# Gate products of a recurrent block: three reduced-precision products of split operands in place of full-precision matmuls, on a two-block model with attention, recurrence, long convolution and experts

## The chip, the cores and the metric

One core of a Trainium2 chip runs the whole forward pass of two model blocks for one sequence of 256 tokens (width 1024). Its engines work side by side, each on its own queue: TensorE (PE; its weight loads are listed as PEld), VectorE (DVE), ScalarE (ACT), GpSimd (POOL) and SyncE (SP, which issues most transfers). The metric is the device time of one execution in microseconds; lower is better.

## The reference, cut to what matters

The first block has two layers (windowed attention with an MLP, then a gated recurrence with an MLP), the second a mix of three token mixers and an expert layer. The change is in the gates of the recurrence. `x` there is 256 x 1536, cut into 16 blocks of 96 channels, and each block has a 96 x 96 matrix for each of two gates and two directions:

```python
def rg_lru(x, w_a, b_a, w_x, b_x, lam, reverse):
    xb = x.reshape(B, S, N_RNN_BLOCKS, RNN_BLOCK_W)
    r = sigmoid(einsum("bsni,nij->bsnj", xb, w_a).reshape(B, S, D_RNN) + b_a)
    i = sigmoid(einsum("bsni,nij->bsnj", xb, w_x).reshape(B, S, D_RNN) + b_x)
    log_a = -LRU_C * r * softplus(-lam)
    a = exp(log_a)
    u = sqrt(-expm1(2.0 * log_a)) * (i * x)
    ...                       # linear scan over time of (a, u)

def recurrent_block(h, w_in, conv_w, conv_b, ..., w_out):
    xr, gate = split(h @ w_in, 2)
    xr = centred_depthwise_conv(xr, conv_w, conv_b)
    y = rg_lru(xr, forward) + rg_lru(xr, reverse)
    return (y * gelu(gate)) @ w_out
```

The second thing the change touches is the spectra of the long-convolution filters of the second block (`Kre`, `Krz`, `Kim`), which depend on weights alone and are computed early.

## The kernel before

Large products are made of three fp32r matmuls each: both operands are split into a high part, rounded by a copy to fp32r on ScalarE, and a low part, the difference, made on VectorE; `mm3` (L388) adds high x high, high x low and low x high. Weights come through one stream `W` (class `Stream`): SyncE loads items of 1 MB into five staging buffers, `split_to` (L219 ScalarE, L224 VectorE) splits them in halves of 1024 columns into four pairs of buffers, `next` hands them out in a fixed order. A scheduler orders each engine's instructions by program order and readiness, except in attention, where TensorE's order is as written. GpSimd issues the small loads (`GP.dma_start`) and does few operations.

The recurrent block (`recurrent`, from L1452) works on four groups of 384 channels, in three tiles of 128 channels by 256 tokens. For each group:

- `gin(g)`: for each tile, 48 matmuls 128x256 of split input and weights give x and the gate branch in one PSUM bank; ScalarE copies them out (L1476, L1477, L1484, L1485), VectorE does the convolution taps (L1479) and the gelu (L1486, L1488). `xr[g]` holds the three x tiles.
- `gates(g)`: 96-channel blocks do not line up with 128-channel tiles, so an output tile `mt` needs the x tiles in `PAIRS[mt]`: the first needs x tiles 0 and 1, the middle one all three, the last 1 and 2. For each direction, output tile and gate, L1503 issues a full-precision (f32) matmul per pair, of the loaded blocks `BD[g % 2]` with zeros around them: 28 in a group, each of which the trace lists as two instructions. Then ScalarE takes two biased tanh, an exp and a tanh for each tile and direction (L1506 to L1509) and a square (L1512); VectorE multiplies (L1513, L1514). After all of them come square roots (L1523), scans over time (L1529, L1531) and the product with the gelu, split into `yH` and `yL` (L1536, L1537).
- `gout(g - 1)`: 36 products 128x512 of the previous group's `yH`, `yL` with output weights, into four accumulator banks. The last group's follow at the end.

The general banks (`gen`) are three in rotation, so a gate product can start only when the bank three before it has been read. For the last group, gates and what follows run tile by tile (`pieces`).

`load_bd(g)` loads a group's gate blocks by 20 small DMAs on GpSimd's queue (L1430) into one of two buffers `BD[0]`, `BD[1]`; groups 0 and 1 are loaded ahead of the first MLP, 2 and 3 after `gates(0)` and `gates(1)`. `run_late(ins)` runs four operations of 128x1024 on the residual (`affine`, L905 and L908), in group 1; they read the tiles `lng`, `lnb`. The filter spectra stay in `Kre`, `Krz`, `Kim` from the end of attention until the second block's convolution. `channel_terms` runs in the middle of the first MLP.

## Time and profile before

| | |
|---|---|
| Time of three runs | 1211.99, 1214.86 (median), 1220.63 us |
| Profiled execution | 1219.98 us, of which the span from first to last instruction is 1218.2 us |
| TensorE busy | 1128.1 us, 93% of the span |
| VectorE busy | 771.6 us, 63% |
| ScalarE busy | 552.4 us, 45% |
| GpSimd busy | 104.2 us, 9% |
| HBM traffic | 315.27 MB read, 1.09 MB written, 260 GB/s over the span |
| Mean granted clock of TensorE | 0.974 |

Busy time is an average over stages: TensorE at 93% does not say which engine ends each stage. So the rows below are cut by stage. The recurrent block runs from about 350 to 528 us of the span, the first MLP from about 153 to 339, the second from about 541. A matmul's duration overlaps that of the next; what it costs is the distance between two starts.

### The profile page before, as it was taken

To read this page: it belongs to the slowest core of one execution; us is meant where nothing else is said; L and a number is where in the kernel's file an instruction comes from. 1 tells how busy PE (TensorE), PEld (TensorE's weight loads), DVE (VectorE), ACT (ScalarE), POOL (GpSimd) and SP (SyncE) were. 2 spreads that over 40 slices of the span, in tenths; PEclk is the share of its full clock that TensorE was granted. 3 is DMA by queue.
4 is the path that set the end of the run, shared out by engine and by line. 5 is a ranking of instruction groups with operands and counts; after the bars stand their busy time and mean duration, and the time that the engine had idled before them with its cause. 6 is when DMAs were issued, how large, how long until landed. Compare 5 with 4: busy or idle time off the path is not lost. (4 is left out here: it accounts for less than half of the span.)

```text
span 1218.2 us, 17320 instructions
## 1 busy us (share of the span) xinstructions
PE 1128.1 (93%) x6610; PEld 822.0 (67%) x6610; DVE 771.6 (63%) x1448; ACT 552.4 (45%) x935; POOL 104.2 (9%) x177
## 2 busy tenths in 40 slices
PE   5999699999989999979999999899999997989884
PEld 3657598988866577558889989899987543334321
DVE  4588688878575786588778879878798511101003
ACT  2456344454467777745345547644656211011101
POOL 6000170000013210010000000100000000000000
PEclk9999889999999999989999999999999899999998
DMA  9988498988694572478779766653346769999993
GB/s 285 327 320 302 175 311 295 337 293 306 205 277 125 168 198 69 143 279 323 261 267 321 270 211 208 209 174 129 100 143 239 284 249 419 417 413 419 420 411 124
DMA packets 147075, 317.58 MB, mean 261 GB/s; under 512 B 8402, under 2 KB 97730, under 8 KB 133672
## 3 DMA queue, kind: packets, MB, share of 16 engines
q1 hardware_dynamic: 139768, 304.17, 69.9%
q0 software_dynamic: 7216, 12.22, 3.2%
q8 instruction: 54, 0.88, 0.3%
q14 instruction: 37, 0.30, 0.1%
HBM read 315.27 MB, written 1.09 MB: 260 GB/s over the span
## 5 line engine op out<-in xcount | busy, mean ns | idle before, releaser
L219 ACT ACTIVATE wh<-stg 128x1024 fp32r<-128x1024 f32 x236 | 241.2, 1042 | 190.2 <-issue 71.9
L224 DVE TENSOR_TENSOR wl<-stg,wh 128x1024 fp32r<-128x1024 f32 x233 | 277.0, 1207 | 75.8 <-ACT wh L219 73.0
L391 PE MATMUL gen<-hH,wh 128*128 128x256 f32 x704 | 198.5, 282 | 4.3 <-ACT hH L851 3.0
L393 PE MATMUL gen<-hH,wl 128*128 128x256 f32 x704 | 197.2, 281 | 5.0 <-DVE wl L224 5.0
L392 PE MATMUL gen<-hL,wh 128*128 128x256 f32 x704 | 196.3, 279 | 1.3 <-DVE hL L855 1.3
L391 PEld LDWEIGHTS gen<-hH,wh 128*128 128x128 f32 x704 | 133.7, 190 | 12.1 <-ACT hH L851 5.7
L393 PEld LDWEIGHTS gen<-hH,wl 128*128 128x128 f32 x704 | 133.8, 190 | 7.9 <-DVE wl L224 7.8
L392 PEld LDWEIGHTS gen<-hL,wh 128*128 128x128 f32 x704 | 133.5, 190 | 3.2 <-POOL zp L1458 1.1
L391 PE MATMUL acc<-wh,mH 128*128 128x512 f32 x256 | 101.3, 396 | 0.0
L393 PE MATMUL acc<-wh,mL 128*128 128x512 f32 x256 | 100.7, 393 | 0.0
L392 PE MATMUL acc<-wl,mH 128*128 128x512 f32 x256 | 100.5, 392 | 0.0
L468 DVE SCALAR_TENSOR_TENSOR adav<-stg,csil,adav 128x1024 f32<-128x1024 f32 (+2 forms) x56 | 79.3, 1415 | 10.2 <-DMA stg<-in_ada_w_dram 9.4
L2423 PE MATMUL mmi<-stg,mhT 128*32 128x512 f32 (+2 forms) x256 | 69.6, 599 | 7.7 <-SPq L2486 3.9
L2395 PE MATMUL mgu<-stg,wh 128*32 128x512 f32 (+2 forms) x256 | 66.6, 648 | 5.9 <-DMA stg<-in_moe_w_up_dram 5.9
L2395 PE MATMUL mgu<-stg,wl 128*32 128x512 f32 (+2 forms) x256 | 65.1, 595 | 7.2 <-DMA stg<-in_moe_w_up_dram 7.2
L2400 DVE SCALAR_TENSOR_TENSOR mhid<-mgu,mws,mhid 128x512 f32<-128x512 f32 x7 | 5.3, 750 | 93.8 <-PE mgu L2395 93.8
L1503 PE MATMUL gen<-xr,bd 128*128 128x256 f32 (+1 forms) x224 | 60.3, 410 | 1.4 <-DVE xr L1479 1.4
L2428 ACT ACTIVATE wh<-mmi 128x512 fp32r<-128x512 f32 x14 | 8.4, 598 | 111.7 <-PE mmi L2423 111.7
L2423 PEld LDWEIGHTS mmi<-stg,mhT 128*32 128x32 f32 (+2 forms) x256 | 20.2, 129 | 54.5 <-issue 36.2
L2429 DVE TENSOR_TENSOR wl<-mmi,wh 128x512 fp32r<-128x512 f32 x14 | 9.7, 692 | 74.0 <-ACT wh L2428 74.0
L391 PEld LDWEIGHTS acc<-wh,mH 128*128 128x128 f32 x256 | 48.1, 188 | 11.7 <-ACT mH L1310 0.8
L393 PEld LDWEIGHTS acc<-wh,mL 128*128 128x128 f32 x256 | 48.1, 188 | 11.0 <-issue 0.8
(597 smaller groups left out, 2160.0 us busy)
## 6 DMA issues: line engine op xcount, KB each, us to landing
stg<-in_ada_w_dram SPq DMA_DIRECT2D x72, 1024.0 KB, 6.1
stg<-in_mlp_w_dram SPq DMA_DIRECT2D x64, 1024.0 KB, 6.5
stg<-in_moe_w_up_dram SPq DMA_DIRECT2D x32, 1024.0 KB, 16.3
stg<-in_moe_w_gate_dram SPq DMA_DIRECT2D x32, 1024.0 KB, 15.2
stg<-in_moe_w_down_dram SPq DMA_DIRECT2D x32, 1024.0 KB, 18.8
stg<-in_w_in_dram SPq DMA_DIRECT2D x20, 1024.0 KB, 5.4
stg<-in_rnn_w_in_dram SPq DMA_DIRECT2D x12, 1024.0 KB, 6.3
stg<-in_attn_w_in_dram SPq DMA_DIRECT2D x8, 768.0 KB, 10.4
```

What stands on the lines that cost most here:

```text
L219: nc.scalar.activation(h, t[:, sl], AF.Copy)
L224: sub()
L391: PE.matmul(o, ah, bh, start=first, stop=False)
L392: PE.matmul(o, ah, bl, start=False, stop=False)
L393: return PE.matmul(o, al, bh, start=False, stop=last)
L468: V.scalar_tensor_tensor(acc, tv[:, j, :], col[:, k:k + 1], acc, op0=OP.mult, op1=OP.add)
L1503: PE.matmul(pv[c0:c1, q, :], BD[g % 2][:, q, d, o:o + c1 - c0], xr[g][:, kt, :], start=(i == 0), stop=True, skip_group_check=True)
L2395: PE.matmul(ps[sl], gx[c][:, k, o + sl.start:o + sl.stop], t[:, 512 * k:512 * k + 512], start=first, stop=last)
L2400: V.scalar_tensor_tensor(hid, got[1], WS[w], hid, op0=OP.mult, op1=OP.mult)
L2423: PE.matmul(ps[h][sl], hT[:, 2 * c + k, sl], t[:, 1024 * k + 512 * h:1024 * k + 512 * h + 512], start=c == 0 and k == 0, stop=c == 1 and k ...
L2428: SC.activation(yH[:, h, :], ps[h], AF.Copy)
L2429: V.tensor_sub(yL[:, h, :], ps[h], yH[:, h, :].bitcast(F32))
```

## The change

The gate matrices and the x tiles are split like the other operands, and the gate products become three fp32r products each.

- `split_bd(g)`: ScalarE copies the loaded blocks (two halves of 1280 columns) to `BDH`, GpSimd subtracts to get `BDL`, then the next group's load is issued. `BD`, `BDH`, `BDL` exist once each. Group 0's split stands at the end of `channel_terms`, the others' after the second tile of `gin(g)`.
- x is split after each tile of `gin`: copies on ScalarE, the low part on GpSimd for the first two tiles and on VectorE for the third. A fourth, mixed tile holds channels 32 to 127 of x tile 0 and 0 to 31 of x tile 2, so that the middle output tile needs two contractions and not three. The split tiles live in the buffers `lng` and `lnb`; `run_late` therefore moves to the first tile of group 0.
- The layout `SLOT` gives every piece the full 128 output columns (640 columns in all), and an output tile takes two pieces (`MINE`): one over 128 rows and, for the first and last tile, one over 64 rows, in different halves of the array; six pieces a group. The products of output tiles 0 and 2 alternate, then tile 1 follows.
- `gout(g - 1)` becomes a generator: its first 6 of 12 steps are placed after direction 0 of `gates(g)`, the rest after direction 1.
- The spectra lie in one tile `KK`, which is written to DRAM (`parked`) when they are complete and read back after the recurrent block; its 10 KB a partition are free in between.

The diff without the unchanged and the purely renamed parts:

```diff
@@ -947,9 +947,18 @@
     sks = ExitStack()
     sxp = ctx.enter_context(tc.tile_pool(name="sx", bufs=1, side="right", reuse_waits="tile"))
     skp = sks.enter_context(tc.tile_pool(name="sk", bufs=1, side="right", reuse_waits="tile"))
-    Kre = skp.tile([128, 2, 2, 256], F32, name="Kre")
-    Krz = skp.tile([128, 2, 256], F32, name="Krz")
-    Kim = skp.tile([128, 2, 2, 256], F32, name="Kim")
+
+    def filters(pool):
+
+
+        KK = pool.tile([128, 2560], F32, name="KK")
+        return (KK, KK[:, 0:1024].rearrange("p (k o c) -> p k o c", k=2, o=2),
+                KK[:, 1024:1536].rearrange("p (o c) -> p o c", o=2),
+                KK[:, 1536:2560].rearrange("p (k o c) -> p k o c", k=2, o=2))
+
+    KK, Kre, Krz, Kim = filters(skp)
+    parked = ctx.enter_context(tc.tile_pool(name="park", bufs=1, space=bass.MemoryType.DRAM)).tile(
+        [128, 2560], F32, name="parked")
...
         hps.close()
+        GP.dma_start(parked, KK)
+        sks.close()
...
@@ -1405,29 +1416,33 @@
         V.tensor_scalar(hb[:, 0], CV("b_a"), 0.5, None, op0=OP.mult)
         V.tensor_scalar(hb[:, 1], CV("b_x"), 0.5, None, op0=OP.mult)
         yield
-
-
-    SLOT, o = {}, 0
-    for key, c0, c1 in (((0, 0), 0, 128), ((1, 0), 96, 128), ((1, 1), 0, 128), ((0, 1), 0, 64), ((2, 1), 64, 128),
-                        ((2, 2), 0, 128), ((1, 2), 0, 32)):
-        SLOT[key] = (o, c0, c1)
-        o += c1 - c0
+        split_bd(0)
+        yield
+
+
+    SLOT = {(0, 0): 0, (1, 1): 128, (2, 2): 256, (1, 0): 384, (1, 2): 384, (0, 1): 512, (2, 1): 512}
     bds = ExitStack()
     bdp = bds.enter_context(tc.tile_pool(name="bd", bufs=1, reuse_waits="tile"))
-    BD = []
-    for b_ in range(2):
-        bd = bdp.tile([128, 2, 2, 576], F32, name=f"bd{b_}")
-        GP.memset(bd[:, 0], 0.0)
-        GP.memset(bd[:, 1], 0.0)
-        BD.append(bd)
+    BD = bdp.tile([128, 2, 2, 640], F32, name="bd")
+    GP.memset(BD[:, 0], 0.0)
+    GP.memset(BD[:, 1], 0.0)
+    BDH = bdp.tile([128, 2, 2, 640], F32R, name="bdH")
+    BDL = bdp.tile([128, 2, 2, 640], F32R, name="bdL")
+
+    def split_bd(g):
+        for q in range(2):
+            SC.activation(BDH[:, q], BD[:, q], AF.Copy)
+            GP.tensor_sub(BDL[:, q], BD[:, q], BDH[:, q].bitcast(F32))
+        if g < 3:
+            load_bd(g + 1)
 
     def load_bd(g):
         for q, n in enumerate(("rnn_w_a", "rnn_w_x")):
             src = A[n][0].rearrange("d n i j -> i n d j")
 
             def put(key, p0, p1, c0, c1, b, i0, j0):
...
     load_bd(0)
-    load_bd(1)
...
+                if g == 0 and j == 0:
+                    run_late(ins)
+                if j == 0:
+                    xs[g] = [lnp.tile([128, D], F32, name=n, bufs=1).bitcast(F32R).rearrange(
+                        "p (j n) -> p j n", j=4) for n in ("lng", "lnb")]
+                xH, xL = (v[:, j, :] for v in xs[g])
+                SC.activation(xH, u, AF.Copy)
+                (V if j == 2 else GP).tensor_sub(xL, u, xH.bitcast(F32))
+
+                mH, mL = (v[:, 3, :] for v in xs[g])
+                if j == 0:
+                    SC.activation(mH, u, AF.Copy)
+                    GP.tensor_sub(mL, u, mH.bitcast(F32))
+                if j == 2:
+                    SC.activation(mH[0:32], u[0:32], AF.Copy)
+                    V.tensor_sub(mL[0:32], u[0:32], mH[0:32].bitcast(F32))
+                if g and j == 1:
+                    split_bd(g)
+
+        def gates(g, between):
             pieces = [slice(0, 3)] if g < 3 else [slice(i, i + 1) for i in range(3)]
             tr, ti, aa = [[rw.tile([128, 3, 256], F32, name=n) for _ in range(2)] for n in ("tr", "ti", "aa")]
+
+            MINE = {0: ((0, 0, 128, 0), (384, 0, 64, 1)), 1: ((128, 0, 128, 1), (512, 0, 128, 3)),
+                    2: ((256, 0, 128, 2), (384, 64, 128, 1))}
+
+            def products(ps, d, mts):
+
+                for q in range(2):
+                    for part in range(2):
+                        for x, y_ in ((BDH, 0), (BDH, 1), (BDL, 0)):
+                            for mt in mts:
+                                o, p0, p1, j = MINE[mt][part]
+                                PE.matmul(ps[mt][:, 256 * q:256 * q + 256], x[p0:p1, q, d, o:o + 128], xs[g][y_][p0:p1, j, :],
+                                          start=part == 0 and x is BDH and not y_, stop=part == 1 and x is BDL)
+
             for pc in pieces:
                 for d in range(2):
-                    for mt in range(pc.start, pc.stop):
-                        ps = gen()
-                        pv = ps.rearrange("p (m n) -> p m n", m=2)
-                        c = 12 * d + 3 * g + mt
-                        for q in range(2):
-                            for i, kt in enumerate(PAIRS[mt]):
-                                o, c0, c1 = SLOT[kt, mt]
-                                PE.matmul(pv[c0:c1, q, :], BD[g % 2][:, q, d, o:o + c1 - c0], xr[g][:, kt, :],
-                                          start=(i == 0), stop=True, skip_group_check=True)
-                        r, u, e = tr[d][:, mt], ti[d][:, mt], aa[d][:, mt]
-                        SC.activation(r, pv[:, 0, :], AF.Tanh, bias=hb[:, 0, c:c + 1], scale=0.5)
-                        SC.activation(u, pv[:, 1, :], AF.Tanh, bias=hb[:, 1, c:c + 1], scale=0.5)
-                        SC.activation(e, r, AF.Exp, bias=sn4[:, c:c + 1], scale=sn4[:, c:c + 1])
-                        SC.activation(r, r, AF.Tanh, bias=sp4[:, c:c + 1], scale=sp4[:, c:c + 1])
+                    ps = {}
+                    for banks in ((0, 2), (1,)) if g < 3 else ((pc.start,),):
+                        for mt in banks:
+                            ps[mt] = gen()
+                        products(ps, d, banks)
+                        for mt in banks:
+                            c = 12 * d + 3 * g + mt
+                            pv = ps[mt].rearrange("p (m n) -> p m n", m=2)
+                            r, u, e = tr[d][:, mt], ti[d][:, mt], aa[d][:, mt]
+                            SC.activation(r, pv[:, 0, :], AF.Tanh, bias=hb[:, 0, c:c + 1], scale=0.5)
+                            SC.activation(u, pv[:, 1, :], AF.Tanh, bias=hb[:, 1, c:c + 1], scale=0.5)
+                            SC.activation(e, r, AF.Exp, bias=sn4[:, c:c + 1], scale=sn4[:, c:c + 1])
+                            SC.activation(r, r, AF.Tanh, bias=sp4[:, c:c + 1], scale=sp4[:, c:c + 1])
+                    next(between, None)
 
                     q = rw.tile([128, 3, 256], F32, name="sq", bufs=1)
                     last = SC.activation(q[:, pc], aa[d][:, pc], AF.Square)
                     V.scalar_tensor_tensor(tr[d][:, pc], q[:, pc], 1.0, tr[d][:, pc], op0=OP.add, op1=OP.mult)
                     V.scalar_tensor_tensor(ti[d][:, pc], ti[d][:, pc], 1.0, xr[g][:, pc], op0=OP.add, op1=OP.mult)
-            if g < 2:
-                load_bd(g + 2)
...
-            for m, t, h in order:
+            for n, (m, t, h) in enumerate(order):
+                if n == 6:
+                    yield
                 wh, wl = cur[m // 2](m % 2)
                 ts, hs = slice(128 * t, 128 * t + 128), slice(512 * h, 512 * h + 512)
                 mm3(y[t][h], (H[:, m - 3 * g, ts], L[:, m - 3 * g, ts]), (wh[:, hs], wl[:, hs]), m == 0, m == 11)
 
         for g in range(4):
-            ins = gin(g)
-            if g == 1:
-                run_late(ins)
-            gates(g)
-            if g:
-                gout(g - 1)
-        gout(3)
+            gin(g)
+            out = gout(g - 1) if g else iter(())
+            gates(g, out)
+            for _ in out:
+                pass
+        for _ in gout(3):
+            pass
...
+    sks = ExitStack()
+    skp = sks.enter_context(tc.tile_pool(name="sk2", bufs=1, side="right", reuse_waits="tile"))
+    KK, Kre, Krz, Kim = filters(skp)
+    GP.dma_start(KK, parked)
```

## Rows read from the trace of the kernel before

**Rows 1.** Busy time by stage: stretch, length, busy us (instructions), clock, DMA share, GB/s
```profile
350.50:527.50 177.00, 171.60 (x1006) 117.99 (x1010) 123.21 (x191) 127.39 (x234) 27.14 (x48) 1.00 0.55 169
...
368.80:384.40 15.60, 15.60 (x66) 5.56 (x64) 6.04 (x9) 11.82 (x26) 4.91 (x9) 1.00 0.64 208
...
384.40:428.10 43.70, 41.61 (x246) 29.16 (x246) 32.50 (x44) 34.02 (x61) 17.03 (x30) 1.00 0.45 128
428.10:471.50 43.40, 42.88 (x246) 29.67 (x245) 29.16 (x46) 31.42 (x56) 3.81 (x7) 1.00 0.55 162
...
471.50:490.60 19.10, 17.44 (x148) 16.71 (x146) 17.90 (x28) 13.91 (x22) 0.00 (x0) 1.00 0.33 110
250.00:335.00 85.00, 85.00 (x541) 73.22 (x540) 63.40 (x92) 38.67 (x46) 1.35 (x2) 1.00 0.78 264
```

The columns after the length are TensorE, its weight loads, VectorE, ScalarE, GpSimd.

**Rows 2.** Page, costliest groups: line, operation, shape, count, busy us, mean ns, idle before
```profile
L1503 PE MATMUL gen<-xr,bd 128*128 128x256 f32 (+1 forms) x224 | 60.3, 410 | 1.4 <-DVE xr L1479 1.4
```

**Rows 3.** Timeline of TensorE: start us, length us, line, operation, shape, count
```profile
480.00 0.29 PE L391 MATMUL gen<-hH,wh 128*128 128x256 f32 x1
...
483.87 0.28 PE L392 MATMUL gen<-hL,wh 128*128 128x256 f32 x1
...
498.50 8.21 PE L1503 MATMUL gen<-xr,bd 128*64 128x256 f32 x32
...
506.99 0.40 PE L392 MATMUL acc<-wl,yH 128*128 128x512 f32 x1
...
514.92 0.40 PE L393 MATMUL acc<-wh,yL 128*128 128x512 f32 x1
```

**Rows 4.** ScalarE: two groups by line, and its timeline in group 3's gates
```profile
L219 ACT ACTIVATE wh<-stg 128x1024 fp32r<-128x1024 f32 x36 | 37.8, 1059 | 18.8 <-PE gen L392 12.0 <-PE acc L393 4.7 <-DMA stg<-in_mlp_w_dram 2.1
...
L1476 ACT ACTIVATE zp<-gen 128x256 f32<-128x256 f32 x12 | 4.4, 370 | 0.4 <-PE gen L393 0.4
...
501.61 0.46 ACT L1507 ACTIVATE ti<-gen,hb 128x256 f32<-128x256 f32 x1
...
503.61 0.47 ACT L1507 ACTIVATE ti<-gen,hb 128x256 f32<-128x256 f32 x1
```

**Rows 5.** VectorE: two groups by line, 343 to 528 us
```profile
L224 DVE TENSOR_TENSOR wl<-stg,wh 128x1024 fp32r<-128x1024 f32 x35 | 42.3, 1218 | 8.6 <-ACT wh L219 8.2
...
L1537 DVE TENSOR_TENSOR yL<-tr,yH 128x256 fp32r<-128x256 f32 x3 | 1.3, 417 | 0.5 <-ACT yH L1536 0.5
```

**Rows 6.** Timelines of GpSimd and VectorE; line L855 on both: ns min/median/max, starts
```profile
147.45 3.69 POOL L855 TENSOR_TENSOR hL<-tv,hH 128x512 fp32r<-128x512 f32 x2 [16.26 <-ACT hH L851]
...
147.72 2.30 DVE L224 TENSOR_TENSOR wl<-stg,wh 128x1024 fp32r<-128x1024 f32 x1
...
L855 POOL TENSOR_TENSOR hL<-tv,hH x6: 1262/1267/2238, 147.5 to 539.9; 128x512 fp32r<-128x512 f32 x6
L855 DVE TENSOR_TENSOR hL<-tv,hH x6: 677/682/1183, 152.7 to 543.1; 128x512 fp32r<-128x512 f32 x6
```

**Rows 7.** Timelines of ScalarE and VectorE around the gates of group 0
```profile
371.69 1.00 DVE L1479 SCALAR_TENSOR_TENSOR xr<-zp,chv,xr 128x256 f32<-128x256 f32 x2
...
386.84 0.83 ACT L1512 ACTIVATE sq<-aa 128x768 f32<-128x768 f32 x1
```

**Rows 8.** Timeline of ScalarE in group 3's gates; in brackets the idle time before
```profile
500.44 0.47 ACT L1506 ACTIVATE tr<-gen,hb 128x256 f32<-128x256 f32 x1 [3.99 <-PE gen L1503]
```

**Rows 9.** Stretches as in rows 1, and a TensorE wait from its timeline
```profile
346.00:349.00 3.00, 0.97 (x7) 0.58 (x5) 2.44 (x7) 2.20 (x6) 0.38 (x1) 1.00 0.95 360
...
149.00:152.00 3.00, 0.18 (x2) 0.00 (x1) 2.79 (x6) 2.17 (x6) 3.00 (x2) 0.51 0.00 0
...
533.00:536.00 3.00, 2.46 (x11) 2.10 (x12) 2.65 (x9) 1.58 (x4) 0.00 (x0) 0.50 0.96 325
...
533.54 0.88 PE L842 MATMUL gen<-csm,xnat 128*128 128x128 f32 x3 [4.23 <-DVE bmv L878]
```

9 lines of the change are left out of this document (3 added, 6 removed).

## The prediction

> **What bounds the kernel now.** I read the busy time by stage first. The recurrent block, the stage that the change edits, is 177.0 us long, and TensorE is busy for 171.6 of them; ScalarE for 127.4, VectorE for 123.2, GpSimd for 27.1 [rows 1]. TensorE is the bound, at full clock, and the other two have some 50 us to spare each. Next, the group of the gate products: 112 full-precision matmuls, each listed as two instructions, keep TensorE busy for 60.3 us [rows 2]. Last, the timeline, for the pitch at which matmuls follow each other (a duration overlaps the next one's). The 128x256 products of split operands run from 480.00 to 483.87 in 34 steps: 3.87 / 34 = 0.114 us each. The gate products of the last group, 32 instructions in 8.21 us, take 0.257 us each, so 0.514 a matmul. The output products, 128x512, run from 506.99 to 514.92 in 34 steps: 0.233 us each [rows 3].
>
> **The gate products.** The new loop issues, for each of four groups and two directions, 3 column blocks x 2 gates x 2 pieces x 3 products = 36 matmuls, 288 in all. At 0.114 us they take 32.8 us in place of 60.3: TensorE is rid of 27.5 us, or 6.9 a group (15.1 to 8.2). 96 of the 288 contract over 64 rows only, a form for which before has no row. If two of them ran at once (72 can pair, in groups 0 to 2) that would save 36 x 0.114 = 4.1 us more; if each cost as much as a full-precision one, 96 x (0.514 - 0.114) = 38.4 us would be lost. I take 0.114: they move the same 256 columns in the same format.
>
> **What the split adds.** ScalarE: five copies a group (three of x, two for the mixed tile), at 0.37 us as the 128x256 copy, and two of the gate weights, 1280 wide, at 1.06 x 1.25 = 1.32 us [rows 4]. That is 1.85 + 2.64 = 4.5 us a group. The weight split of group 0 falls into the first MLP, so the stage gets 4 x 1.85 + 3 x 2.64 = 15.3 us, and ScalarE comes to 142.7.
> VectorE: two 128x256 subtractions a group at 0.42 us, 0.8 us [rows 5], 3.3 in all.
> GpSimd: three 128x256 subtractions and two of 1280 columns. Its own 128x512 subtraction takes 1.267 us [rows 6], so by width 3 x 0.63 + 2 x 3.17 = 8.2 us a group, and 12 x 0.63 + 6 x 3.17 = 26.6 us in the stage.
>
> **These 26.6 us are not free.** At 147.45 GpSimd begins two subtractions. VectorE's 128x1024 subtraction that begins at 147.72 takes 2.30 us, not the usual 1.22, and the GpSimd pair takes 3.69, not 2 x 1.27. VectorE's own 128x512 subtraction has a median of 0.682 and a maximum of 1.183, GpSimd's 1.267 and 2.238 [rows 5, 6]. So they take turns: VectorE waits until the first has ended at 148.7 and then needs its 1.2, and GpSimd's second waits for that. I therefore add the two engines up as one resource: 123.2 + 3.3 + 26.6 = 153.1 us. That is now the longest of the three, ahead of TensorE (171.6 - 27.5 = 144.1) and ScalarE (142.7).
> The Trainium skill (SBUF — State Buffer, "Who interferes with whom") says why: a VectorE instruction with two inputs in SBUF and a GpSimd instruction that reads SBUF share one port, held for the whole instruction, and the loser fully blocks. The trace agrees (2.30 us). Without that rule VectorE would stand at 126.5 and not count; with it, one 3.17 us subtraction can hold a weight split up for as long.
>
> **Group by group.** Group 0: there is no output product yet to fill a wait. The input products end at 368.8, the gates at 384.4, 15.6 us later [rows 1]. Before, column block 0 starts at once since it needs only two of the three x tiles; now the first banks hold blocks 0 and 2, which need the third. That tile is finished by VectorE at 372.7 (371.69 + 1.00) [rows 7]; a copy (0.37) and a subtraction (0.42) bring it to 4.7 us after the end of the input products. Then 24 products (2.7 us) for two banks and 12 (1.4) for the third. There are three banks, so direction 1 waits for ScalarE to empty two: the first gate is complete at 6.1, and a block costs ScalarE 2.0 us with its square, 1.7 without [rows 4]; after two biased tanh of the second block, at about 9.6, TensorE goes on and ends at 13.7. So 1.9 us of 6.9 are gained, and ScalarE ends its last square at 18.9, as it does now (386.84 + 0.83) [rows 7].
> Groups 1 and 2: the wait for the third x tile is covered by the first half of the previous group's output products, 18 x 0.233 = 4.2 us, which need nothing new. The periods from one group's input products to the next one's are 43.7 and 43.4 us [rows 1]. In the first, ScalarE comes to 34.0 + 4.5 = 38.5, VectorE and GpSimd to 32.5 - 4.9 + 0.8 + 8.2 = 36.6 (the four 1.22 us operations on the residual move to group 0), TensorE to 34.7. In the second ScalarE has 35.9, VectorE and GpSimd 29.2 + 9.0 = 38.2, TensorE 36.0. Before, the period exceeded its busiest engine by 2.1 and 0.5 us; I add 1.5 and get 40.0 and 39.7: a gain of 3.7 each.
> Group 3: gates and output are a chain over ScalarE and VectorE. ScalarE waits 3.99 us in it for gate products [rows 8]; that goes, and two copies (0.74) come. I take 3.0.
> Sum: 1.9 + 3.7 + 3.7 + 3.0 = 12.3, so 12 us.
>
> **What I cost at nothing.** The split of group 0's gate weights in the first MLP (2.6 us of ScalarE, 6.3 of GpSimd): TensorE is busy 85.0 of 85 us there and VectorE 63.4 [rows 1], so the 6.3 us fit in its 21.6 idle ones; uncovered they would cost those 6.3. The affine of the residual, moved to group 0 (4.9 us of VectorE): in the gates of group 0 VectorE has 9.5 idle of 15.6 us [rows 1]. The write of the spectra, 1.31 MB: its data are complete when attention ends, and from 149 to 152 the DMA engines move nothing [rows 9]; if it met weight loads it would take 4.0 us at 325 GB/s [rows 9]. The read back falls between recurrent block and second MLP, on GpSimd's queue, ahead of the context rows; at worst the same 4.0 us. Twenty fewer weight loads ahead of the first MLP are off the path. The loads of the next group's gate weights sit behind the split on GpSimd's queue; the next thing queued there is a subtraction some 25 us later. The split buffers are single now, so the split waits for the previous group's gates, which TensorE has passed by then.
>
> **Rivals.** (a) Everything overlaps: the stage falls to its busiest resource, 153.1 plus 2 us: 22 us gained, 1193. For it: before, TensorE was used at 97%. Against it: then one engine was full, now three are close. (b) The GpSimd subtractions collide where VectorE is already full. The input products of group 3 last 19.1 us with VectorE busy 17.9 [rows 1]; 8.2 + 0.8 more make 26.9, 7.8 longer, against 6.9 that the gates give back, so groups 1 to 3 gain nothing and lose 0.9 each: -1.9 + 2.7 = +0.8, about 1215. For it: the 3.17 us pieces are released just there, in the middle of the input products, and the weight splits that feed TensorE are what would wait. Against: VectorE can split ahead while the gates run. The skill's port rule, that the loser waits for a whole instruction, speaks for this rival. (c) Slower: TensorE's waits ahead of the gates cost it its clock. After a wait of 4.23 us the granted clock is 0.50 in 533 to 536, that is 1.2 GHz, and it is 0.51 in 149 to 152; in 346 to 349, with 0.97 us busy in short waits, it stays 1.00, 2.4 GHz [rows 9]. If the split of x and weights is late by 3 us or more in a group, that wait and some 9 us at half clock (4.5 lost) cost 7.5 us; it decides only if it happens in all four groups: -12 + 30 = +18, 1233. Against: output products fill the wait in three of them. (d) The change does not do what it says: the 96 products over 64 rows cost as much as full-precision ones. Then TensorE is the bound again with 144.1 + 38.4 = 182.5 us, and with the 5.4 us that it idles now (177.0 - 171.6) the stage takes 187.9, 11 more than now: 1226. The 0.114 us of the same format and width in the same stage speaks against it, so I give it no chance of its own beside (c).
>
> **Numbers.** The sum is made within a profiled execution of 1219.98 us, whose span is 1218.2; it ran 0.4% above the median of the runs, 1214.86. The 12 us are taken off that median: 1203, with a range of its own of 1196 to 1210. Chances: this forecast 0.45, (a) 0.20, (b) 0.25, (c) and (d) 0.10. The range that leaves out (c) and the far end of (a) is 1188 to 1219. A measurement of this kernel tells about 1%, 12 us, from no change, and the forecast lies on that line: faster by over 1% (below 1202.7) is (a) and half of the forecast, 0.43; within 1% the other half and (b), 0.47; slower 0.10.
>
> **What would show it.** In the profile after: the gate matmuls at a pitch of 0.114 us and some 33 us busy (if not, (d)); ScalarE's and VectorE's shares of the stage up to nine tenths; a TensorE wait of 3 to 5 us ahead of the gates of group 0; in groups 1 and 2 periods near 40. VectorE weight splits of well over 1.22 us beside GpSimd's subtractions and TensorE waiting for the low halves of the weights would show (b); a clock of 0.50 inside the stage (c). The forecast is wrong if the stage isn't 165 us, or if stages outside it move by more than 3.

## The result: 2.9% slower, and where the time is in the profile after

The changed kernel takes 1252.61 us (median of 4 runs, 1245.66 to 1255.57) against 1216.44 for the kernel before on the same chip: a ratio of 1.029, 95% interval 1.0255 to 1.0325. The forecast was 1203, with 1188 to 1219 as its range.

The profiled execution after took 1245.66 us, the shortest of the four. In it the first input products of the recurrent block start at 355.86 us (before 350.56, 5.3 later), the block lasts 206.4 us (before 176.9, from its first input product to its last output product: 29.5 more), and the rest takes 681.6 in place of 690.7. In the profiles of all kernels whose expert layer does the usual amount of work that rest lies between 681.6 and 695.1 us, so the 9.1 us say nothing of the change. I go by the block and by what lies ahead of it; their 29.5 and 5.3 us make 34.8, and the medians differ by 36.2.

The busy time by stage, with the columns of [rows 1]: length, TensorE, its weight loads, VectorE, ScalarE, GpSimd, granted clock, DMA share, GB/s. The stretches are the input products of group 0, its gates, groups 1 and 2, the input products of group 3, and its gates with the output; the last line is the whole block.

```profile
355.86:374.30 18.44, 18.44 (x150) 18.44 (x147) 15.28 (x20) 13.07 (x22) 2.00 (x3) 0.93 0.84 261
374.30:395.80 21.50, 16.87 (x82) 12.93 (x80) 9.46 (x14) 10.18 (x23) 1.65 (x2) 0.68 0.49 147
395.80:444.00 48.20, 40.72 (x261) 34.96 (x261) 34.95 (x42) 38.38 (x72) 21.66 (x25) 0.89 0.35 100
444.00:493.00 49.00, 42.62 (x262) 36.51 (x261) 34.30 (x47) 34.42 (x63) 25.19 (x27) 0.90 0.48 141
493.00:522.00 29.00, 20.68 (x156) 19.41 (x154) 26.38 (x30) 19.40 (x30) 11.75 (x5) 0.88 0.31 112
522.00:562.30 40.30, 35.60 (x183) 25.12 (x181) 25.95 (x53) 24.74 (x54) 1.65 (x3) 0.92 0.66 237
355.86:562.30 206.44, 174.94 (x1084) 147.37 (x1080) 146.33 (x202) 140.19 (x259) 63.90 (x64) 0.88 0.49 158
```

Beside [rows 1] the gates of group 0 take 21.5 us in place of 15.6, groups 1 and 2 take 48.2 and 49.0 in place of 43.7 and 43.4, and the input products of group 3 take 29.0 in place of 19.1. The last stretch takes 40.3; before it was 36.9 (490.6 to the block's end at 527.5). No stage gained. TensorE's busy time did not fall either (174.9 beside 171.6), though it has less to do: the clock of the block is 0.88 where it was 1.00.

What TensorE waited for in the block (engine, operation, line, the work it waited for, us in total, times, longest):

```profile
PE acc L391 <- ACT yH L1578: 11.5, 3, 6.8
PE gen L1535 <- ACT lng L1508: 10.0, 4, 6.2
PE gen L1535 <- POOL lnb L1509: 4.1, 2, 2.9
PE gen L393 <- DVE wl L224: 3.3, 3, 2.2
```

The names: `yH` is the high half of the gated output of the group before, `lng` and `lnb` are the new high and low halves of `x`. Two thirds of the idle time (21.5 of 31.5 us) is spent waiting for two copies that ScalarE makes, `yH` and `lng`. After such waits the clock is 0.50, that is 1.2 GHz: in the gates of group 0 and in the middle of group 3's input products, for example:

```profile
382.00:392.00 10.00, 9.38 (x35) 7.81 (x35) 1.11 (x3) 2.78 (x8) 0.00 (x0) 0.50 0.49 148
...
513.00:519.00 6.00, 5.00 (x23) 5.01 (x24) 6.00 (x9) 4.82 (x11) 3.08 (x2) 0.50 0.40 142
```

The block can therefore be split into three parts. I took stretches of 1 us and summed busy time times clock (the work, as it would be at full clock), busy time times one minus clock (lost to the clock), and idle time. The same for every kernel that was run (e4, with the gates of before, and e7, which differs ahead of the block, left out):

| kernel | block us | work at full clock | lost to clock | idle |
|---|---|---|---|---|
| before | 176.9 | 171.6 | 0.0 | 5.4 |
| forecast (its own numbers) | 165 | 144.1 | 0 | 20.9 |
| after | 206.4 | 154.9 | 20.0 | 31.5 |
| e1 gate weights split once | 194.8 | 154.8 | 14.3 | 25.7 |
| e2 subtractions on VectorE | 192.5 | 155.1 | 18.2 | 19.2 |
| e3 x split once | 196.6 | 154.6 | 18.5 | 23.5 |
| e5 TensorE in written order | 219.6 | 143.8 | 24.8 | 50.9 |
| e6 both split once | 183.4 | 154.0 | 11.7 | 17.6 |
| e8 subtraction in pieces | 219.5 | 155.8 | 20.7 | 43.0 |
| e9 one fp32r product of three | 187.6 | 136.0 | 18.0 | 33.5 |
| e10 one full-precision product | 203.0 | 159.3 | 16.6 | 27.2 |
| e11 wait of group 0 filled | 200.5 | 159.9 | 13.7 | 26.8 |
| e12 three losses mended | 185.0 | 159.8 | 8.7 | 16.6 |
| e13 last outputs behind the gates | 201.1 | 154.9 | 19.0 | 27.3 |
| e14 e12 and e13 together | 179.0 | 159.8 | 5.1 | 14.1 |
| e15 e12, all outputs behind the gates | 186.6 | 161.7 | 10.5 | 14.4 |

The work of e11, e12, e14 and e15 holds 5.3 us (46 x 0.114) of idle products. The change took 16.7 us of work from TensorE and gave it 20.0 us of half clock and 26.1 us of idle time: +29.4.

**The chain that makes TensorE wait**, in the input products of group 3. Timelines of GpSimd, VectorE, ScalarE and TensorE (start, length, engine, line, operation, count; in brackets the idle time before and what ended it):

```profile
503.10 7.12 POOL L1435 TENSOR_TENSOR bdL<-bd,bdH 128x1280 fp32r<-128x1280 f32 x2 [28.85 <-ACT bdH L1434]
...
504.30 3.18 DVE L1492 SCALAR_TENSOR_TENSOR xr<-zp,chv,xr 128x256 f32<-128x256 f32 x1
507.39 3.63 DVE L1577 SCALAR_TENSOR_TENSOR tr<-tr,ge 128x768 f32<-128x768 f32 x1
...
512.95 1.21 DVE L224 TENSOR_TENSOR wl<-stg,wh 128x1024 fp32r<-128x1024 f32 x1
...
511.06 0.84 ACT L1578 ACTIVATE yH<-tr 128x768 fp32r<-128x768 f32 x1 [6.88 <-DVE tr L1577]
...
513.54 0.40 ACT L1508 ACTIVATE lng<-xr 128x256 fp32r<-128x256 f32 x1
...
514.00 0.58 PE L1535 MATMUL gen<-lng,bdH 128*128 128x256 f32 x1 [6.16 <-ACT lng L1508]
514.37 0.42 PE L393 MATMUL gen<-hH,wl 128*128 128x256 f32 x1
```

GpSimd's two 1280-wide subtractions hold VectorE: the convolution tap that takes 0.47 us on average where VectorE does them itself (e2) takes 3.18, the 128x768 product 3.63 in place of 0.95. ScalarE works in order, and its copy `yH` waits 6.88 us for that product; the copy of `x` that a gate product needs stands behind it, at 513.54. VectorE's own subtraction for the next input weights (`wl`) stands behind the two slow instructions as well and ends at 514.16. TensorE works in order too: the gate product needs the one, the input product behind it the other, and so TensorE is idle for 6.16 us and goes on at half clock (the stretch 513 to 519 above). Without the gate product in front it would have waited about as long, for `wl`.

### The profile page after: what moved, and what is told of

Read it like the earlier page. It is cut to its first block, busy times and chain, and to the rows that moved or that the text cites. A ratio compares the mean times of both kernels' runs of the same rounds, so it can differ in the third digit from the quotient of the medians.

```text
span 1243.9 us, 17482 instructions
## 1 busy us (share of the span) xinstructions
PE 1122.5 (90%) x6674; PEld 844.5 (68%) x6674; DVE 795.4 (64%) x1456; ACT 567.3 (46%) x963; POOL 147.8 (12%) x197
## 5 line engine op out<-in xcount | busy, mean ns | idle before, releaser
L224 DVE TENSOR_TENSOR wl<-stg,wh 128x1024 fp32r<-128x1024 f32 x233 | 279.2, 1215 | 84.4 <-ACT wh L219 81.2
L391 PE MATMUL gen<-hH,wh 128*128 128x256 f32 x704 | 203.3, 289 | 8.0 <-ACT hH L851 4.5
L393 PE MATMUL gen<-hH,wl 128*128 128x256 f32 x704 | 202.0, 287 | 4.3 <-DVE wl L224 4.3
L392 PE MATMUL gen<-hL,wh 128*128 128x256 f32 x704 | 201.1, 286 | 0.5 <-DVE hL L855 0.5
L391 PEld LDWEIGHTS gen<-hH,wh 128*128 128x128 f32 x704 | 139.0, 198 | 18.0 <-ACT wh L219 7.5
L393 PEld LDWEIGHTS gen<-hH,wl 128*128 128x128 f32 x704 | 138.9, 197 | 6.4 <-DVE wl L224 6.2
L392 PEld LDWEIGHTS gen<-hL,wh 128*128 128x128 f32 x704 | 138.6, 197 | 2.0 <-issue 0.9
L468 DVE SCALAR_TENSOR_TENSOR adav<-stg,csil,adav 128x1024 f32<-128x1024 f32 (+2 forms) x56 | 79.2, 1415 | 12.5 <-DMA stg<-in_ada_w_dram 11.7
L392 PEld LDWEIGHTS acc<-wl,mH 128*128 128x128 f32 x256 | 48.5, 190 | 10.3 <-DVE wl L224 0.6
## 6 DMA issues: line engine op xcount, KB each, us to landing
stg<-in_moe_w_up_dram SPq DMA_DIRECT2D x32, 1024.0 KB, 16.6
stg<-in_moe_w_down_dram SPq DMA_DIRECT2D x32, 1024.0 KB, 18.8
```

Source lines behind the costliest of these rows:

```text
L224: sub()
L391: PE.matmul(o, ah, bh, start=first, stop=False)
L392: PE.matmul(o, ah, bl, start=False, stop=False)
L393: return PE.matmul(o, al, bh, start=False, stop=last)
L468: V.scalar_tensor_tensor(acc, tv[:, j, :], col[:, k:k + 1], acc, op0=OP.mult, op1=OP.add)
```

## The experiments

All are edits of the kernel after unless said. A ratio is to the kernel before on the same chip; the block's numbers stand in the table above.

### e1, e3, e6: the split done once

e1 leaves out the load and split of gate weights in groups 1 to 3 (the lines with a minus), e3 the split of `x` in them (those with a plus), e6 both:

```diff
 def split_bd(g):
...
-    if g < 3:
-        load_bd(g + 1)
...
+                if g:
+                    xs[g] = xs[0]
...
+                    continue
...
-                if g and j == 1:
-                    split_bd(g)
```

> Left out: the load and the split of the gate weights of groups 1 to 3; all groups use those of group 0. In the changed kernel the recurrent block takes 206 us (356 to 562) against 177 before. Theory L (the two 1280-wide GpSimd subtractions of a group hold VectorE for 3.0 us each, the split output yH comes late, TensorE stands behind it in issue order and loses its clock): the block falls to about 180 to 188 us, the kernel to about 1228. Theory X (the gates wait for the split of the third x tile, whoever holds VectorE): at most 8 us go, the block stays near 200, the kernel near 1243. Theory M (parking the spectra and the new memory plan cost the time elsewhere): no change beyond 3 us.

> Left out: the split of x in groups 1 to 3, whose gate products use the split x of group 0. Theory X: the waits ahead of the gates of groups 2 and 3 (2.9 and 6.2 us) and the half clock after them vanish, the block falls by 20 us or more, the kernel to about 1230. Theory L: the 3 us subtractions of the gate weights are still there, so yH is still late; the block falls by 10 us at most, to about 197, the kernel to about 1243. Theory M: no change beyond 3 us.

> The kernel after, without the split of x and without the load and split of gate weights in groups 1 to 3: group 0's halves are used in all groups (these values, and so the gates, are not the reference's). All products stay. It leaves out 6.2 us of ScalarE, 3.1 of VectorE and GpSimd for x and 7.9 and 19 us of them for the weights. Theory S (the split's work is the loss): leaving out one of the two parts gave back 10 to 12 us each, both together give back 20 to 24, and the block comes to 182 to 187, still above before's 176.9 only by what group 0 loses (6 us). Rival P (the products are): the products and their grouping in banks cost the rest, both together give no more than one, and the block stays above 192.

Measured: e1 1241.8 us (1.0219, 1.0146 to 1.0292), block 194.8; e3 1241.8 (1.0202, 1.0134 to 1.0269), block 196.6; e6 1230.41 (1.0122, 1.0063 to 1.018), block 183.4. e1's gain lies between theory L's 18 to 26 us and theory X's 8 at most, e3's fits L, e6's fits theory S, and theory M falls. So the weights cost the block 11.6 us, `x` 9.8, both 23.0: the two parts of the split add up, and without them the block is still 6.5 longer than before. Group 0, whose split stays, accounts for that and more: in e6 its gates end 41.7 us after the block's start (396.8 - 355.1), 7.9 later than before. So even without a split groups 1 to 3 gain 1.4 us only. The work on TensorE is the same in all three (154 to 155); it is idle time and clock that come back.

### e2: GpSimd's subtractions on VectorE

```diff
-            GP.tensor_sub(BDL[:, q], BD[:, q], BDH[:, q].bitcast(F32))
+            V.tensor_sub(BDL[:, q], BD[:, q], BDH[:, q].bitcast(F32))
...
-                (V if j == 2 else GP).tensor_sub(xL, u, xH.bitcast(F32))
+                V.tensor_sub(xL, u, xH.bitcast(F32))
...
-                    GP.tensor_sub(mL, u, mH.bitcast(F32))
+                    V.tensor_sub(mL, u, mH.bitcast(F32))
```

> Nothing left out: all subtractions of the splits of x and of the gate weights run on VectorE in place of GpSimd. By width they take 12 x 0.42 + 6 x 1.52 = 14 us there in the block, against 27 us of GpSimd with VectorE shut out. Theory L: VectorE operations of 3 us vanish, the waits of 6.8 and 6.2 us shrink, the block falls to about 185 to 195 us, the kernel to about 1235. Theory X: the waits ahead of the gates become longer, since VectorE is in order: block 205 or more, kernel 1250 to 1260. Theory M: no change beyond 3 us.

Measured: 1237.07 us (1.0158, 1.0089 to 1.0226), block 192.5, 13.9 less than after. Theory L holds and X falls. The block, with the columns as above:

```profile
358.36:550.89 192.53, 173.32 (x1084) 145.98 (x1080) 138.77 (x220) 140.36 (x259) 26.11 (x45) 0.89 0.53 168
```

VectorE's busy time in the block falls, from 146.3 to 138.8 us, although it does all of GpSimd's subtractions now: the time that it spent blocked was more than the work.

### e8: the wide subtraction in pieces

```diff
-            GP.tensor_sub(BDL[:, q], BD[:, q], BDH[:, q].bitcast(F32))
+            for d in range(2):
+                for c in range(0, 640, 160):
+                    v = (slice(None), q, d, slice(c, c + 160))
+                    GP.tensor_sub(BDL[v], BD[v], BDH[v].bitcast(F32))
```

> The kernel after, with each 1280-wide GpSimd subtraction of the gate weights cut into eight of 160 columns: the same work, each lock an eighth as long. Theory L (length of the lock): VectorE's 3 us instructions beside them become 1.2 to 1.5 us, the high halves of the outputs come earlier, and the block gives back about what moving the subtractions to VectorE gave, 10 to 14 us: 193 to 196. Rival T (total): VectorE and GpSimd share the time whatever the length, VectorE's instructions are delayed once per piece, and the block stays within 4 us of 206.

Measured: 1263.96 us (1.0382, 1.0318 to 1.0446), block 219.5, 13 us longer than after: both theories fall. Groups of GpSimd by line (count, busy us, mean ns, idle before), first after, then e8:

```profile
L1435 POOL TENSOR_TENSOR bdL<-bd,bdH 128x1280 fp32r<-128x1280 f32 x6 | 22.1, 3682 | 73.6 <-ACT bdH L1434 73.6
...
L1509 POOL TENSOR_TENSOR lnb<-xr,lng 128x256 fp32r<-128x256 f32 x8 | 12.3, 1534 | 26.5 <-ACT lng L1513 16.4 <-ACT lng L1508 10.0
...
L1514 POOL TENSOR_TENSOR lnb<-xr,lng 128x256 fp32r<-128x256 f32 x4 | 3.5, 874 | 0.0
```

```profile
L1438 POOL TENSOR_TENSOR bdL<-bd,bdH 128x160 fp32r<-128x160 f32 x48 | 43.4, 938 | 75.9 <-ACT bdH L1434 75.9
```

The line of e8 is GpSimd's, and TensorE's first wait shows who paid:

```profile
PE gen L1538 <- POOL lnb L1512: 19.1, 5, 7.3
```

Eight pieces take 7.5 us (8 x 0.938) where one subtraction took 3.7; eight of the shortest would take 4.1 (8 x 0.509, the minimum of the line). VectorE is hardly relieved (144.6 us busy in the block, after 146.3). I read this as GpSimd being held now, piece by piece, and it is in order: the low half of `x`, which TensorE needs, stands behind the pieces.

### e5: TensorE in written order

```diff
-    y = recurrent(hH, hL)
+    with tc.manual_schedule(engines={mybir.EngineType.PE}):
+        y = recurrent(hH, hL)
```

> The kernel after, but with TensorE's instructions of the recurrent block issued in the order in which the program writes them: no output product stands ahead of the next group's input products. Theory O (order): the waits of 6.8 and 6.2 us in groups 1 and 2 arise because one output product, or one gate product, was put ahead of input products that were ready; in program order those input products fill the time, TensorE's idle time in the block (31.5 us after) falls to some 18, with about 5 us less of half clock, and the block goes from 206.4 to about 190. Rival B (a shared bound): ScalarE and VectorE set the pace of the groups and TensorE only waits elsewhere: the wait moves to the gates or to the outputs behind them, and the block stays at 202 or more.

Measured: 1270.97 us (1.0445, 1.0388 to 1.0502), block 219.6. The order that the scheduler chose is better than the written one by 13 us; theory O falls. The waits move to other places, and grow:

```profile
PE gen L393 <- DVE wl L224: 21.8, 5, 8.9
PE gen L1535 <- ACT lng L1508: 16.6, 3, 6.8
PE acc L391 <- ACT yH L1578: 10.4, 2, 8.9
```

The input products, put first, wait for `wl` in their turn, as the one in the chain above does.

Its work, though, is 143.8 us, and the forecast had 144.1. That is in part luck, since 18 fewer products of modulation fills than before fell into its block (44 for 62). Counted from start to start (to a product's end where TensorE then idles, times the clock), the fills take 5.1 us there and 9.5 before. But the gate products are cheaper too: 37.4 us, 0.130 each, where after's take 42.2, 0.147 each. The timelines of TensorE show why, first after, then e5 (a line with x2 is two products):

```profile
425.71 0.28 PE L1535 MATMUL gen<-lng,bdH 128*128 128x256 f32 x1
425.83 0.28 PE L1535 MATMUL gen<-lnb,bdH 128*128 128x256 f32 x1
425.95 0.28 PE L1535 MATMUL gen<-lng,bdL 128*128 128x256 f32 x1
426.16 0.38 PE L1535 MATMUL gen<-lng,bdH 64*128 64x256 f32 x1
426.38 0.28 PE L1535 MATMUL gen<-lnb,bdH 64*128 64x256 f32 x1
426.50 0.28 PE L1535 MATMUL gen<-lng,bdL 64*128 64x256 f32 x1
426.71 0.38 PE L1535 MATMUL gen<-lng,bdH 128*128 128x256 f32 x1
```

```profile
441.52 0.39 PE L1535 MATMUL gen<-lng,bdH 128*128 128x256 f32 x2
441.75 0.40 PE L1535 MATMUL gen<-lnb,bdH 128*128 128x256 f32 x2
441.99 0.40 PE L1535 MATMUL gen<-lng,bdL 128*128 128x256 f32 x2
442.32 0.39 PE L1535 MATMUL gen<-lng,bdH 64*128 64x256 f32 x2
...
442.87 0.50 PE L1535 MATMUL gen<-lng,bdH 128*128 128x256 f32 x2
```

In e5 banks 0 and 2 go together: twelve products from 441.52 to 442.87, 0.113 us each. After, the scheduler had put one bank behind the other: six from 425.71 to 426.71, 0.167 each. The pitch is 0.12 within a kind and 0.21 to 0.22 twice at every step from products over 128 rows to products over 64 and back. In e5 the two products of a pair over 64 rows start together, and that makes up for these steps; all 36 pairs do so there, only 15 after. The Trainium skill (TensorEngine Tiling (Array Packing), "Key Properties") says that changing the tiling mode drains TensorE; the trace agrees, with some 0.2 us for each change.

### e9, e10: less and more work for TensorE, beside the same split

Both keep only the product of the low halves, which waits for everything that the three products wait for. The diff is e9's; in e10 both operands are read as F32 besides.

```diff
-                        for x, y_ in ((BDH, 0), (BDH, 1), (BDL, 0)):
+                        for x, y_ in ((BDL, 1),):
...
-                                PE.matmul(ps[mt][:, 256 * q:256 * q + 256], x[p0:p1, q, d, o:o + 128], xs[g][y_][p0:p1, j, :],
-                                          start=part == 0 and x is BDH and not y_, stop=part == 1 and x is BDL)
+                                PE.matmul(ps[mt][:, 256 * q:256 * q + 256], x[p0:p1, q, d, o:o + 128], xs[g][y_][p0:p1, j, :],
+                                          start=part == 0, stop=part == 1)
```

> The kernel after, with one gate product of three: only low half times low half, which still needs both halves of the weights and of x to be ready (the other two products are left out, so the gates are not the reference's). All of the split's work stays; TensorE has 192 fp32r products fewer, 192 x 0.139 = 27 us at full clock. Theory C (the block is set by the chain over ScalarE, VectorE and GpSimd that feeds and empties TensorE): the block stays within 10 us of after's 206. Rival T (TensorE still sets it): the block falls by 20 us or more, to 186 or below.

> The kernel after, with the three fp32r products of split operands replaced by one full-precision product of the low halves (the gates are not the reference's): the split's work and every wait on it stay, TensorE has 96 products of 0.514 us, 49 us, where after has 288 of 0.139, 40 us. Theory C (the chain over the other engines sets the block): within 10 us of after's 206, like the kernel with one fp32r product of three; what the three products save on TensorE is then worth little even beside the same split. Rival T (TensorE sets it): the block is 9 us longer than after's and 30 or more longer than that of the kernel with one fp32r product.

The expert layer's work depends on its input, and with these gates it runs twice as many weight products (512 in place of 256), so the whole times (1494.44 and 1512.84 us) say nothing here. The block of each:

```profile
355.88:543.44 187.56, 154.06 (x892) 122.87 (x888) 142.24 (x203) 136.97 (x257) 62.70 (x67) 0.88 0.57 177
```

```profile
357.05:560.08 203.03, 175.87 (x988) 136.82 (x984) 136.69 (x198) 138.53 (x256) 58.66 (x64) 0.90 0.51 162
```

e9 is 18.8 us shorter than after with 18.9 us less work. Theory C falls, and T's 20 us nearly come: here TensorE's work counts one for one, although TensorE idles for 33.5 us. I read this as a ring: TensorE waits for a half, the engine that makes the half waits for TensorE's products in its turn, so work and waits stand in a row, and a saving on either counts. That is not shown, for e10 doesn't fit it: with 4.4 us more work than after it is 3.4 us shorter (3.4 less at half clock, 4.3 less idle), and 15.4 longer than e9 where T had 30. Why stays open. What it does say is that beside this split the three products are worth no more than one full-precision product.

### e11: the wait of group 0 filled

```diff
+                        if g == 0 and d == 0 and 2 in banks:
+                            for _ in range(46):
+                                PE.matmul(ps[2][:, 0:256], hH[:, 0, 0:128], hL[:, 0, :], start=True, stop=True)
                         products(ps, d, banks)
```

> The kernel after, with 46 idle fp32r products of 256 columns (5.3 us at full clock; their result is overwritten) ahead of the gate products of group 0, in the place where TensorE waits for the third tile's split. Theory K (the clock is what group 0 loses): the granted clock stays at 1.00 from 374 to the end of the gates, the products that ran at half clock from 382.6 to 392 take half as long, and the gates of group 0 end 4 to 5 us earlier after the end of the input products (17 us in place of 21.5). Rival A (ScalarE sets group 0's end): with the products early ScalarE becomes the bound again and the gates' end moves by less than 1.5 us.

Measured: 1246.62 us (1.0264, 1.0236 to 1.0293), block 200.5. The idle products run from 374.55 to 380.07, and the gates of group 0 end 36.8 us after the block's start, in place of 40.0: 3.2 earlier, short of K's 4 to 5 and above A's 1.5. From the end of the input products they take 18.4 us at a clock of 0.81, where after's took 21.5 at 0.68 (374.30 to 395.80 above). The clock does not stay at 1.00, as K had it: a wait of 1.40 us for the third tile is left.

```profile
376.60:395.00 18.40, 17.00 (x105) 14.72 (x104) 8.82 (x14) 10.13 (x24) 1.55 (x1) 0.81 0.39 115
```

So about half of what group 0 lost (6.2 us, 40.0 beside 33.8 before) was the clock behind a wait that was itself forecast. The other 2.7 of the block's 5.9 us lie behind group 0.

### e4, e7: ahead of the block

e4 is the kernel before with the parking of the spectra alone; e7 is the kernel after with one order changed, of the VectorE work that a modulation fill needs:

```diff
-            V.tensor_sub(Lf, r, Hf.bitcast(F32))
+            low = V.tensor_sub(Lf, r, Hf.bitcast(F32))
+            if b == 0:
+                W.fourth = [2, low.ins]
...
+                if self.fourth and not self.fourth[0]:
+                    es.enter_context(self.tc.issue_after(self.fourth[1]))
+                if self.fourth:
+                    self.fourth[0] -= 1
```

> The kernel before with one part of the change alone: the filter spectra are written to DRAM after attention and read back after the recurrent block. Theories L and X: within 2 us of the kernel before (1214 to 1219), the block 177 us. Theory M: the first MLP starts with a wait of some 4 us for weights, as in the changed kernel, and the kernel takes 1221 to 1225.

> The kernel after, but the third of the modulation fills that run beside the first MLP may start on VectorE only after the first block's subtraction for its low half; in the kernel after it stood in front of it and waited 5.6 us for its load. Theory V (order on VectorE): TensorE's wait of 4.1 us in the first MLP goes, and the first input products of the recurrent block start 4 to 6 us earlier, at about 350 to 352; total 1247 to 1249. Rival D (the parked write takes the transfer time): 1.31 MB more in the queues make the weights late by about 4 us, TensorE waits for them instead, and the input products start at 355 as they do now.

e4: 1225.25 us (1.0075, 1.0045 to 1.0105), its block unchanged at 176.8 but begun 9.1 us later. So parking has no part in what the block lost, but the total comes out as theory M had it (1221 to 1225). M's wait in the first MLP is there too; it is not for weights, though, but for `mL`, the low half of an activation. VectorE and TensorE, the kernel before, then e4:

```profile
165.90 0.68 DVE L1311 TENSOR_TENSOR mL<-mr,mH 128x512 fp32r<-128x512 f32 x1
...
170.43 1.28 DVE L468 SCALAR_TENSOR_TENSOR adav<-stg,csil,adav 128x1024 f32<-128x1024 f32 x1 [0.26 <-DMA stg<-in_ada_w_dram]
```

```profile
171.50 1.28 DVE L468 SCALAR_TENSOR_TENSOR adav<-stg,csil,adav 128x1024 f32<-128x1024 f32 x1 [6.70 <-DMA stg<-in_ada_w_dram]
172.70 0.69 DVE L1322 TENSOR_TENSOR mL<-mr,mH 128x512 fp32r<-128x512 f32 x1
...
173.44 0.80 PE L393 MATMUL acc<-wh,mL 128*128 128x512 f32 x1 [6.68 <-DVE mL L1322]
```

With the parking alone a fill stands ahead of `mL`, where before it stood behind. In e4 the read back is issued early, at 150.17, because its room isn't used again; in the kernel after it comes behind the block.

e7: 1250.61 (1.0282, 1.0223 to 1.034), its block begins at 352.20, 3.7 us before that of after. VectorE and TensorE in the first MLP, first after, then e7:

```profile
168.56 1.28 DVE L468 SCALAR_TENSOR_TENSOR adav<-stg,csil,adav 128x1024 f32<-128x1024 f32 x1 [5.62 <-DMA stg<-in_ada_w_dram]
169.76 0.68 DVE L1322 TENSOR_TENSOR mL<-mr,mH 128x512 fp32r<-128x512 f32 x1
...
170.50 0.53 PE L393 MATMUL acc<-wh,mL 128*128 128x512 f32 x1 [4.10 <-DVE mL L1322]
```

```profile
164.71 3.49 DVE L1327 TENSOR_TENSOR mL<-mr,mH 128x512 fp32r<-128x512 f32 x1 [2.61 <-ACT mH L1326]
168.35 1.29 DVE L473 SCALAR_TENSOR_TENSOR adav<-stg,csil,adav 128x1024 f32<-128x1024 f32 x1 [0.16 <-DMA stg<-in_ada_w_dram]
...
168.25 0.50 PE L398 MATMUL acc<-wh,mL 128*128 128x512 f32 x1 [2.79 <-DVE mL L1327]
```

After, a fill whose load has not landed stands ahead of `mL`, and VectorE waits 5.62 us for it. With the order put right the fill's load is there when its turn comes. But `mL` now takes 3.49 us in place of 0.68: it meets the split of group 0's gate weights on GpSimd (128x1280, 2.92 us from 164.72), which the forecast had let run in the idle time there. So TensorE still waits 2.79 us, in place of 4.10. With this order the wait is 2.78 in e12, e14 and e15 as well; in the other edits of the kernel after it is 3.9 to 5.5. Theory V holds for the place and not for the size: the order is worth 1 to 3 us. The blocks of e12, e14 and e15 begin at 354.99 to 355.73, those of the kernels without this order at 354.56 to 358.36, so most of e7's 3.7 us is a difference between executions. The difference of the whole times, 2 us, is below what the runs can tell.

### e12 to e15: how far the mending goes

e12 puts three cures together: the subtractions inside the block on VectorE, e7's order, and e11's idle products. e13 is the kernel after, e14 is e12, with the last change undone in group 3: the output products of group 2 come behind the gate products of group 3. The diff is that of e13 and e14; e15 is e12 with `gates(g, iter(()))`, the same in all groups.

```diff
-            gates(g, out)
+            gates(g, out if g < 3 else iter(()))
```

> The kernel after with three of its losses mended together: GpSimd's subtractions inside the recurrent block on VectorE, the third modulation fill behind the first block's low half in the first MLP, and 46 idle products in group 0's wait. If the three losses are separate they add up: 14 us (VectorE) + 4 (fill order, in the first MLP) + 4 (clock) = 22, the block at 188 and the total at 1230, still slower than before. If they share a cause (the late chain) the block stays at 192 or above.

> The kernel after, but in the last group the output products of the group before are written behind all gate products, as in the kernel before, and not between them. Theory G (their place): ScalarE waits less for gate products in the last group and the stretch from the end of its input products to the end of the block, 40.3 us after (36.9 before), falls by 3 to 5 us; total 1248 to 1250. Rival S (the split of x is late there): the gate products wait for the third tile instead, and the stretch stays within 1.5 us of 40.3.

> The kernel with three losses mended (block 185.0 us, total 1229.5), and the output products of the second last group behind the last group's gate products as well. Theory G: the last stretch (499.6 to 540.0 there, 40.4 us) falls by 3 to 5 us, the block to 181, the total to 1225 to 1227, still slower than before. Rival S: within 1.5 us of 40.4.

> As the kernel with three losses mended, but in all groups the output products are written behind the group's gate products, as in the kernel before. If the half of them that the change puts between the gate products covers the wait for the third tile (as the forecast took it), groups 1 and 2 lose 2 to 4 us each and only the last gains: block 187 to 191. If the place of the outputs costs more than it covers, all three gain and the block comes to 175 to 180, about before's 176.9.

Measured: e12 1229.51 us (1.0144, 1.01 to 1.0188), block 185.0, 21.4 less than after: the causes add up in the block (13.9 + 5.9 from e2 and e11 alone is 19.8). The 4 us ahead of it did not show, as said above.

e13: from the end of group 3's input products to the end of the block 34.3 us (524.5 to 558.8) in place of 40.3; e14: 36.2 (498.3 to 534.5) in place of 40.4. Theory G holds for this stretch. ScalarE's waits for gate products, first after, then e13:

```profile
530.24 0.48 ACT L1549 ACTIVATE tr<-gen,hb 128x256 f32<-128x256 f32 x1 [2.02 <-PE gen L1535]
...
536.06 0.48 ACT L1549 ACTIVATE tr<-gen,hb 128x256 f32<-128x256 f32 x1 [2.60 <-PE gen L1535]
```

```profile
532.60 0.47 ACT L1549 ACTIVATE tr<-gen,hb 128x256 f32<-128x256 f32 x1 [0.61 <-PE gen L1535]
```

Yet the whole times stay: e13 1252.03 us (1.0307, 1.0269 to 1.0344), e14 1229.69 (1.0128, 1.0083 to 1.0174). In the profiles the stretch from the block's end to the end of the second MLP takes 6.8 us longer than without the edit, both times (209.0 beside 202.2, and 207.4 beside 200.6); e15 has 207.8. Of e14's 6.8, 2.3 are a longer wait of TensorE for the normalization and 2.0 one for split weights; what makes both later stays open. e15: 1232.71 (1.0139, 1.0096 to 1.0182), block 186.6. It is 7.6 longer than e14's, but 4.4 of that is one wait for the load of a modulation fill, which e14 does not have; the 3.2 that are left for groups 1 and 2 lean to the forecast's view that the outputs cover a wait there, and are too few to settle it.

No version beat the kernel before. e14's block of 179.0 us is still 14 over the forecast's 165: its work without the idle products is 154.5 us (144.1 forecast), the idle products take 5.3, the half clock 5.1, and it idles for 14.1 where the forecast left 20.9.

## Why the prediction was wrong

What happened is its own rivals (b) and (c) together. It added up each engine's work and took the largest sum; in the runs the block became shorter when work left ScalarE, VectorE and GpSimd (e1, e3), moved from GpSimd to VectorE (e2) or left TensorE (e9). Of the 41.4 us between forecast (165) and block (206.4), 10.8 are work, 20.0 clock and 10.6 idle time.

- **Work of the gate products: 27.5 us less was forecast.** Counted from start to start, they took 58.8 us before and take 42.2 after, 0.147 each: 16.6 less. The 60.3 of [rows 2] is a busy time, which counts the overlapping end of every run of products; by the pitch that the prediction had read itself it would be 112 x 0.514 = 57.6. The larger error is the new price. The 0.114 of [rows 3] is nearly met where two banks go together (e5), but only because there the saving by pairs, which the sum left out, makes up for the changes between 128 and 64 rows, some 0.2 us each, which it did not know. After, the scheduler or the single banks of group 3 part the pairs, and the changes are paid without the saving. Rival (d) is off the table.
- **The clock: nothing in the sum, 20.0 us measured.** The prediction knew the price (rival (c), 7.5 us a group) and forecast waits of 3 to 5 us ahead of group 0's gates. They came, as 0.75, 1.23 and 2.66 us; the clock fell from 1.00 to 0.50 at 379.1, behind the second, and rose at 392.8. (c) had priced some 9 us at half clock, for which it showed no row; here it was 13.7. The sum for group 0 had the wait and not the clock. That was the first step that failed: a wait of TensorE was charged its own length only. (c) was to decide only with a late split in all four groups, because outputs fill the wait in three. They don't, since the outputs wait for the same late chain (`yH`, 11.5 us).
- **Two engines as one resource.** The sum of 153.1 us for VectorE and GpSimd was a bound on throughput, and the forecast added 1.5 us a group to it. But the subtractions of GpSimd take 37.9 us in the block (22.1 + 12.3 + 3.5) where 26.6 were forecast: a 128x256 one takes 0.75 us at its shortest, not 0.63, so the width does not scale, and those of L1509 take 1.53 on average. And they come where [rows 1] showed VectorE busy for 17.9 of 19.1 us. Rival (b) put the loss in group 3's input products at 7.8 us; it is 9.9. It came to 1215 and no more because it had neither the clock nor the gate products' true price. Moving the work to VectorE (e2) gave 13.9 us back. By the forecast's own rule for the periods that would have been worth 2.2 us: in the second period VectorE falls to 34.3 (29.2 + 0.8 + 4.3) and TensorE's 36.0 sets it in place of 38.2, and in the first ScalarE's 38.5 is the largest either way. The Trainium skill's rule on the port (SBUF — State Buffer, "Who interferes with whom"), that the loser fully blocks for the instruction, is borne out by 3.63 us for a 0.95 us product. What the forecast left out is that ScalarE and TensorE, which wait behind the blocked VectorE, are in order too.
- **Group 3: 3.0 us less was forecast, 3.4 more came.** The step that failed is that only ScalarE's wait of 3.99 us [rows 8] would go. There the first two placements of outputs both fall within the first tile, so the change puts all 36 of group 2's outputs ahead of the second tile's gate products, 18 behind each direction. New waits of 2.02 and 2.60 us take the old one's place (e13 gives back 6.0 us of the stretch, 2.8 of them clock: 0.92 after, 1.00 in e13).
- **What was costed at nothing.** Ahead of the block 5.3 us were lost; the forecast said that it would be wrong if a stage outside moved by more than 3. The parking brings a new order of one fill and with it a wait for `mL` (e4; 4.10 us after). The split of group 0's weights fits into VectorE's idle time by sum, but holds `mL` for 2.8 us with the order put right (e7). The two do not add up: they hold the same product. How the rest of the 5.3 us comes about is not shown; the block begins between 354.56 and 358.36 in the kernels with the order of after.
- **What held:** the waits ahead of group 0's gates had the size that was given (4.6 us in all), and the read back behind the block costs nothing that shows (from the block's end to the end of the second MLP 202.2 us, before 202.4). Rival (a) was never near: with no split in groups 1 to 3 (e6) the block is still 183.4.

## What to carry to other kernels

Before work is moved from a full engine to others, follow one item round the ring of engines: where TensorE feeds ScalarE and VectorE and they feed it, idle sums on the others are no cover, and what counts is which instruction stands behind which in each queue. In this block 31.5 us of TensorE's waits came with 20.0 us lost at half clock, so a wait that is forecast belongs into the sum with the clock behind it. Keep GpSimd's two-input work away from the stretch in which VectorE is already busy nine tenths, and keep products over 64 and 128 rows in runs of a kind.
